# Paged attention taken two units at a time, with the rotary keys in a record of their own

## The chip, the cores and the metric

The kernel runs on one core of a Trainium2 chip. The metric is the time of one execution on the device in microseconds (us); three runs of the kernel before took 2031.20, 2032.12 and 2036.46 us, so its median is 2032.12 us. The engines named below are PE (the matrix engine, with PEld for its weight loads), DVE (vector), ACT (scalar), POOL (GpSimd) and SP, whose queue only issues transfers here.

## The reference

The reference is one inference step of a two-layer decoder: 1024 prompt tokens and 64 sample tokens (8 sequences of 8 tokens). The change lies in the attention of the sample tokens in layer 1. Each sequence has a past of 8192 keys, kept in 64 pages of 128 keys that a page table picks out of a pool of 640. A key has 256 latent features (`ckv`), 64 rotary features (`kpe`) and one factor for each of the 8 heads (`ks`):

```python
def mla_scores(q_abs, q_pe, ckv, kpe, ks):
    s = (jnp.einsum('bqhc,bkc->bhqk', q_abs, ckv) + jnp.einsum('bqhr,bkr->bhqk', q_pe, kpe))
    return s * (jnp.transpose(ks, (0, 2, 1))[:, :, None, :] * SM_SCALE)

def step(carry, pages):                       # over blocks of pages, for all sequences b
    m, l, acc = carry
    ck, kp, kk = cache_ckv[pages], cache_kpe[pages], cache_ks[pages]
    s = mla_scores(q_abs, q_pe, ck, kp, kk)
    m_new = jnp.maximum(m, jnp.max(s, axis=-1))
    alpha = jnp.exp(m - m_new)
    p = jnp.exp(s - m_new[..., None])
    l = l * alpha + jnp.sum(p, axis=-1)
    acc = acc * alpha[..., None] + jnp.einsum('bhqk,bkc->bhqc', p, ck)
    return m_new, l, acc
```

## The kernel before

Two streams of work are written by generators and merged by `interleave` (line 1780) into one fixed program order: after each step of the right stream (`fr`, line 1816), steps of the left stream (`fl`, line 1817) are emitted until their estimated costs, the numbers after `yield`, have caught up. Every engine and every queue then runs its own part of that order strictly from front to back. While the right stream does the paged attention (`samp_attn`, line 1051), the left one does the dense work of 768 prompt tokens: layer 0's projections, its output product, and layer 1's projections. It streams weight units (`Stream`, line 276): SP loads a unit two ahead (line 297), ACT and DVE or POOL split it in two parts one ahead (lines 183 and 179), PE uses it in products of 384 columns (lines 189 to 191).

The paged attention has 64 units of 8 pages (512 keys). For a unit `u`:

- `load_rec` (line 1060) has SP read the 8 page numbers from `PTi` into registers (line 1064) and then issue 8 transfers from the page pool (line 1067), one for a page. A page's record holds 128 rows of 384 numbers, 1536 bytes a row: 2 x 128 latent columns, 64 columns of rotary keys (64 features of keys 0 to 63 in the lower 64 rows, of keys 64 to 127 in the upper ones), and 64 columns of key factors. There are `RECB` = 2 buffers of 8 records, so the transfers of unit `u + 2` wait until unit `u` has been combined.
- `scores` (line 1080) makes three pairs of f32 products, each with 128 rows and 64 columns of the array and 512 columns streamed: two over the latent (line 1087), one over the rotary part (line 1089), whose query tile `QPE` has zeros in the 64 rows that don't belong. The two of a pair stand for keys 0 to 63 and 64 to 127 of each page and go to the lower and the upper 64 partitions of one bank.
- `combine` (line 1092, DVE) multiplies by the key factors and takes the running maximum; it is the last reader of the record. `soft` (line 1102, ACT) takes the exponentials once for two units (`CU` = 2).
- `tr` and `trev` (lines 1121 and 1128) transpose the weights on PE and copy them out on ACT; `pv` (line 1137) multiplies them with rows of the latent that POOL gathers by indirect transfers (`load_nat`, line 1069); `pvend` (line 1154) adds to the accumulator. A unit's `tr` and `pv` come two units after its scores.

The loop at line 1193 does, for each `u`: loads of `u + 2`, scores of `u`, a step of other work, `combine`, transposes of `u - 2`, a small step, `soft` for every second unit, `pv` of `u - 2`, a step of other work. Order on SP is thus page loads of one unit, then whatever loads and stores the left stream has emitted, then the page loads of the next unit.

## Time and profile before

| what | value |
|---|---|
| median of three runs | 2032.12 us (2031.20 to 2036.46) |
| the profiled execution: its span, from first to last instruction | 2030.3 us |
| PE busy over the span | 1934.9 us (95%) |
| DVE, ACT, POOL busy over the span | 979.2, 744.7, 669.5 us (48%, 37%, 33%) |
| DMA queue that SP feeds | 172178 packets, 298.75 MB, 44.7% of 16 engines |
| DMA queue that POOL feeds | 20528 packets, 67.26 MB, 10.2% of 16 engines |

The profile's page doesn't count the issuing of transfers as busy time of SP; SP is read from the rows of single lines and of the timeline. A line such as `L1067` is line 1067 of the kernel. In lines with instruction durations the three numbers are the least, the median and the greatest in ns.

### The profile page before, as it was taken

What the parts mean: (1) busy time and instruction counts of PE and PEld (TensorE: products, weight loads), DVE (VectorE), ACT (ScalarE), POOL (GpSimd) and SP (SyncE); (2) the same over time, 40 slices, a digit from 0 to 9 for tenths busy, and PEclk for the clock granted to TensorE, in tenths of its full rate; (3) what the DMA queues carried; (4) which work ended last, traced back from release to release, by engine and by line L of the source; (5) the groups of instructions that cost most, each with busy time, mean ns of one, the idle gap of its engine ahead of it and who ended that gap; (6) DMA issues with size and microseconds to landing.
All of it is one profiled execution on the core that took longest, in us unless ns stands there. A gap on an engine that the chain in (4) does not pass through costs nothing. (4 is left out here: it accounts for less than half of the span.)

```text
span 2030.3 us, 33997 instructions
## 1 busy us (share of the span) xinstructions
PE 1934.9 (95%) x11740; PEld 1619.7 (80%) x11740; DVE 979.2 (48%) x2450; ACT 744.7 (37%) x1499; POOL 669.5 (33%) x589
## 2 busy tenths in 40 slices
PE   6997999999999999999999999999998899999999
PEld 5987998998997867667777765777687687787999
DVE  7659444456644533444323443344456656657300
ACT  6434323333321223333222322333333666667300
POOL 4544433422220223233434324333333334433220
PEclk8999999999999999999999999999999999999999
DMA  6552535442535487687988878877852311114532
GB/s 222 168 198 94 179 117 197 145 143 88 176 131 194 136 266 247 226 303 242 339 298 273 278 259 271 264 254 235 270 178 70 93 57 58 59 46 129 179 96 73
DMA packets 192877, 368.17 MB, mean 181 GB/s; under 512 B 27809, under 2 KB 135585, under 8 KB 191426
## 3 DMA queue, kind: packets, MB, share of 16 engines
q1 hardware_dynamic: 172178, 298.75, 44.7%
q0 software_dynamic: 20528, 67.26, 10.2%
q8 instruction: 93, 1.52, 0.3%
q14 instruction: 78, 0.64, 0.1%
HBM read 331.22 MB, written 34.70 MB: 180 GB/s over the span
## 5 line engine op out<-in xcount | busy, mean ns | idle before, releaser
L1078 POOL DMA_INDIRECT nat<-nat,IX x256 | 274.2, 1071 | 490.4 <-PE pv L1152 422.0
L189 PE MATMUL mm<-xH,whi 128*128 128x384 f32 (+1 forms) x1112 | 372.4, 335 | 9.7 <-ACT whi L183 5.1
L191 PE MATMUL mm<-xH,wli 128*128 128x384 f32 (+1 forms) x1112 | 367.1, 330 | 6.1 <-POOL wli L179 4.2
L190 PE MATMUL mm<-xL,whi 128*128 128x384 f32 (+1 forms) x1112 | 366.9, 330 | 0.8 <-DVE xL L179 0.8
L189 PEld LDWEIGHTS mm<-xH,whi 128*128 128x128 f32 x1112 | 213.8, 192 | 32.2 <-issue 13.3
L183 ACT ACTIVATE whi<-wri 128x1024 fp32r<-128x1024 f32 (+1 forms) x130 | 126.1, 977 | 271.1 <-PE mm L190 202.6
L191 PEld LDWEIGHTS mm<-xH,wli 128*128 128x128 f32 x1112 | 213.6, 192 | 8.3 <-POOL wli L179 5.3
L190 PEld LDWEIGHTS mm<-xL,whi 128*128 128x128 f32 x1112 | 213.8, 192 | 4.1 <-issue 2.4
L179 POOL TENSOR_TENSOR wli<-wri,whi 128x1024 fp32r<-128x1024 f32 (+1 forms) x65 | 146.9, 2264 | 161.2 <-ACT whi L183 161.0
L1087 PE MATMUL sAB<-rec,qar 128*64 128x512 f32 x512 | 153.5, 602 | 0.4 <-DMA rec<-rec 0.2
L1152 PE MATMUL pv<-nat,PT 128*64 128x256 f32 x1024 | 140.9, 392 | 4.8 <-ACT PT L1132 4.0
L1152 PEld LDWEIGHTS pv<-nat,PT 128*64 128x64 f32 x1024 | 75.6, 138 | 55.4 <-issue 13.5
L179 DVE TENSOR_TENSOR wli<-wri,whi 128x1024 fp32r<-128x1024 f32 (+1 forms) x65 | 72.8, 1124 | 72.1 <-ACT whi L183 69.9
L189 PE MATMUL mm<-nH,whi 128*128 128x384 f32 x304 | 105.6, 347 | 0.5 <-issue 0.5
L190 PE MATMUL mm<-nL,whi 128*128 128x384 f32 x304 | 102.4, 338 | 0.0
L191 PE MATMUL mm<-nH,wli 128*128 128x384 f32 x304 | 102.3, 337 | 0.0
L179 POOL TENSOR_TENSOR wlo<-wro,who 128x768 fp32r<-128x768 f32 (+3 forms) x30 | 59.2, 1978 | 118.0 <-ACT who L183 117.9
L189 PE MATMUL mm<-yHo,who 128*128 128x384 f32 (+1 forms) x288 | 97.1, 337 | 0.9 <-ACT yHo L183 0.9
L183 ACT ACTIVATE who<-wro 128x768 fp32r<-128x768 f32 (+3 forms) x44 | 38.1, 873 | 155.9 <-PE mm L190 117.7
L191 PE MATMUL mm<-yHo,wlo 128*128 128x384 f32 (+1 forms) x288 | 94.3, 327 | 0.0
L190 PE MATMUL mm<-yLo,who 128*128 128x384 f32 (+1 forms) x288 | 93.9, 326 | 0.0
L1089 PE MATMUL sAB<-rec,QPE 128*64 128x512 f32 x256 | 91.2, 596 | 0.0
(595 smaller groups left out, 4336.9 us busy)
## 6 DMA issues: line engine op xcount, KB each, us to landing
rec<-rec SPq DMA_DIRECT2D x512, 192.0 KB
wri<-wi SPq DMA_DIRECT2D x114, 512.0 KB
wro<-wo SPq DMA_DIRECT2D x29, 384.0 KB
smkv<-ckm SPq DMA_DIRECT2D x16, 512.0 KB
smkv<-cvm SPq DMA_DIRECT2D x16, 512.0 KB
wrm<-memw SPq DMA_DIRECT2D x7, 1024.0 KB
wro<-wo SPq DMA_DIRECT2D x7, 768.0 KB
yld<-d_ys SPq DMA_DIRECT2D x8, 544.0 KB
```

What stands on the lines that cost most here:

```text
L179: eng.tensor_tensor(out=out, in0=a, in1=h.bitcast(F), op=ALU.subtract)
L183: A.activation(h, src, AF.Copy)
L189: T.matmul(out, wh, xh, start=first, stop=False)
L190: T.matmul(out, wh, xl, start=False, stop=False)
L191: T.matmul(out, wl, xh, start=False, stop=last)
L1078: G.indirect_dma_start(out=t[:, j % 2, :], out_offset=None, in_=I["nat"], in_offset=bass.IndirectOffsetOnAxis(ap=IX[:, q:q + 1], axis=0), ...
L1087: T.matmul(o, QA[:, cb, b, :], t[:, :, cb * 128 + ab * 64:cb * 128 + ab * 64 + 64], start=(cb == 0), stop=False)
L1089: T.matmul(o, QPE[:, b, ab, :], t[:, :, 256:320], start=False, stop=True)
L1152: T.matmul(d["v"][64 * ab:64 * ab + 64, 0:256], PT[:, j, ab, :], n[j][:, ab * 256:ab * 256 + 256], start=(i == 0 and j == 0), stop=(i == C ...
```

## The change

- The record of a page loses its rotary columns: 128 rows of 320 numbers (1280 bytes). The rotary keys become a tensor of their own, `kpr`, with 64 rows of 128 keys (512 bytes a row) for each page.
- `load_rec` issues two transfers for each page: 64 rows of `kpr` into the lower half (first unit of a pair) or the upper half (second unit) of a tile that both units of the pair share, and then the record. There are three buffers of records (`RECB` = 3) and two of the new tile. The load of unit `u + 3` is written behind `combine` of unit `u`.
- `scores` takes both units of a pair: the latent products of the first, those of the second (each as before), and then the four rotary products, each with 64 rows and 64 columns: rows 0 to 63 for the first unit, rows 64 to 127 for the second, two column halves each, into the two units' own banks. `QPE` holds the same queries in both halves, without zeros.
- The loop runs over 32 pairs: scores of both, other work, `combine` and next page load for both, `soft` (now always ahead of the transposes), a small step, transposes and copies of both units of the pair before, a small step, `pv` of both with the gathers that reuse their buffers, other work. The costs after `yield` are those of two units before (5.5 + 0.5 + 0.5 + 4.5 against twice 3.0 + 0.5 + 2.0).
- The second unit's transposes use a bank of the tag `s`; the page table is kept in the spare partition of the tile of own-key weights; the scratch that POOL's indirect transfers use is set to 2048 bytes a partition.
- The comments that the diff removes are left out here.

```diff
-RECB = 2
+RECB = 3
@@ samp_prep
-        QPE = pk.tile([128, DB, 2, 64], F, name="QPE")
-        G.memset(QPE, 0.0)
-        PsT = pk.tile([NS, DB, NS], F, name="PsT")
+        QPE = pk.tile([128, DB, 64], F, name="QPE")
+        PsP = pk.tile([128, DB * NS], F, name="PsP")
+        PsT = PsP[0:NS].rearrange("p (b k) -> p b k", b=DB)
...
-        PTi = pk.tile([1, DB * NPG], I32, name="PTi")
+        PTi = PsP[NS:NS + 1, :].bitcast(I32)
...
-        V.tensor_copy(QPE[0:64, :, 0, :], qpf)
-        A.activation(QPE[64:128, :, 1, :], qpf, AF.Copy)
+        V.tensor_copy(QPE[0:64], qpf)
+        A.activation(QPE[64:128], qpf, AF.Copy)
@@ samp_attn, load_rec
+            c, j = u // CU, u % CU
             with tc.issue_after(regs["last"]):
                 v = nc.values_load_multi_w_load_instructions(PTi[0:1, 8 * u:8 * u + 8], engines=[ET.SP], min_val=0, max_val=NPOOL - 1)[1]
-            t = raw[u] = prec.tile([128, 8, 384], F, name="rec", tag="rec", bufs=RECB)
+            if j == 0:
+                kpr[c] = prec.tile([128, 8, 128], F, name="kpr", tag="kpr", bufs=2)
+            t = raw[u] = prec.tile([128, 8, 320], F, name="rec", tag="rec", bufs=RECB)
             for i in range(8):
+                S.dma_start(out=kpr[c][64 * j:64 * j + 64, i, :], in_=I["kpr"][bass.ds(v[i], 1), :, :].rearrange("o p f -> (o p) f"))
                 regs["last"] = S.dma_start(out=t[:, i, :], in_=I["rec"][bass.ds(v[i], 1), :, :].rearrange("o p f -> (o p) f")).ins
@@ scores
-        def scores(u):
-            b = u // UB
-            s = pst("s", "sAB")
-            t = raw[u]
-            for cb, ab in ((cb, ab) for cb in range(3) for ab in range(2)):
-                o = s[64 * ab:64 * ab + 64, :]
-                if cb < 2:
-                    T.matmul(o, QA[:, cb, b, :], t[:, :, cb * 128 + ab * 64:cb * 128 + ab * 64 + 64], start=(cb == 0), stop=False)
-                else:
-                    T.matmul(o, QPE[:, b, ab, :], t[:, :, 256:320], start=False, stop=True)
-            return s
+        def scores(c, kp):
+            b = CU * c // UB
+            ss = [pst("s", "sAB") for _ in range(CU)]
+            for j, s in enumerate(ss):
+                t = raw[CU * c + j]
+                for cb in range(2):
+                    for ab in range(2):
+                        T.matmul(s[64 * ab:64 * ab + 64, :], QA[:, cb, b, :], t[:, :, cb * 128 + ab * 64:cb * 128 + ab * 64 + 64], start=(cb == 0), stop=False)
+            for j, s in enumerate(ss):
+                q = slice(64 * j, 64 * j + 64)
+                for ab in range(2):
+                    T.matmul(s[64 * ab:64 * ab + 64, :], QPE[q, b, :], kp[q, :, 64 * ab:64 * ab + 64], start=False, stop=True)
+            return ss
@@ tr
-            tp = pst("t", "ptp")
+            tp = pst("s" if i else "t", "ptp")
@@ the loop
-        load_rec(0)
-        load_rec(1)
-        load_nat(0)
+        for u in range(RECB):
+            load_rec(u)
+        for u in range(CU):
+            load_nat(u)
         yield
-        for u in range(NU + LAG):
-            pu = u - LAG
-            load_rec(u + 2)
-            if u < NU:
-                s = scores(u)
-                yield 3.0
-                combine(u, s)
-                if u == NU - 1:
-                    RP.close(1)
-                    yield "T"
-            if pu >= 0:
-                load_nat(pu + 1)
-                PT = trev(pu, tr(pu))
-            yield 0.5
-            if u % CU == CU - 1 and u < NU:
-                soft(u // CU)
-            if pu >= 0:
-                pv(pu, PT)
-                yield 2.0
-                pvend(pu)
+        NC = NU // CU
+        for c in range(NC + 1):
+            us = range(CU * c, CU * c + CU)
+            pus = range(CU * c - CU, CU * c)
+            if c < NC:
+                ss = scores(c, kpr.pop(c))
+                yield 5.5
+                for u, s in zip(us, ss):
+                    combine(u, s)
+                    load_rec(u + RECB)
+                if c == NC - 1:
+                    RP.close(1)
+                    yield "T"
+                soft(c)
+            yield 0.5
+            if c:
+                PT = [trev(u, tr(u)) for u in pus]
+                yield 0.5
+            if c:
+                for u, x in zip(pus, PT):
+                    pv(u, x)
+                    load_nat(u + CU)
+                yield 4.5
+                pvend(pus[-1])
@@ prepare and kernel
-    rec = np.empty((NPOOL, 128, 384), np.float32)
+    rec = np.empty((NPOOL, 128, 320), np.float32)
...
+    a["kpr"] = C(i["cache_kpe"].transpose(0, 2, 1))
...
-    nc = _bacc.Bacc("TRN2", target_bir_lowering=False, num_devices=1)
+    nc = _bacc.Bacc("TRN2", target_bir_lowering=False, num_devices=1, dynamic_dma_scratch_size=2048)
```

## Rows read from the trace of the kernel before

**Rows 1.** Windows: PE, PEld, DVE, ACT, POOL busy, clock, DMA share, GB/s.
```profile
700.00:1455.00 755.00, 743.67 (x4294) 530.18 (x4293) 301.79 (x856) 239.54 (x566) 257.65 (x254) 0.99 0.81 267
```
**Rows 2.** Line 1067, the page transfers on SP: durations in ns, first and last start.
```profile
L1067 SPq FUSED_REGOPS  x512: 2/37/701, 698.3 to 1454.6; - x171
L1067 SPq MOVE rec<-rec x512: 3/29/676, 698.4 to 1454.7; - x171
L1067 SPq DMA_DIRECT2D rec<-rec x512: 2/333/1260, 700.3 to 1454.8; - x171
```
**Rows 3.** Timeline of SP: start, us, operation; page transfers of one unit and of two.
```profile
1070.30 3.96 SPq L1067 DMA_DIRECT2D rec<-rec  x8
...
1148.95 11.53 SPq L1067 DMA_DIRECT2D rec<-rec  x16
```
**Rows 4.** Waits of SP's queue, 700 to 1456 us: total, times, longest.
```profile
SPq L1067 <- DVE mx L1097: 52.1, 20, 8.1
...
SPq L440 <- ACT mqH L183: 0.2, 1, 0.2
```
**Rows 5.** Issues of one transfer on SP: 64 rows, 128 rows, 8 rows.
```profile
L882 SPq DMA_DIRECT2D d_kp<-kpT x8: 485/569/1248, 444.9 to 1272.7; - x8
...
L1253 SPq DMA_DIRECT2D lraw<-d_ck x2: 327/378/430, 1481.5 to 1518.6; - x2
...
L1253 SPq DMA_DIRECT2D lraw<-d_kp x1: 494/494/494, 1526.1 to 1526.1; - x1
...
L1329 SPq DMA_DIRECT2D aqr<-d_qp x8: 450/453/487, 1580.0 to 1775.6; - x8
...
L1374 SPq DMA_DIRECT2D out_ksT<-akt x8: 303/303/343, 1589.8 to 1845.2; - x8
```
**Rows 6.** Transfers issued from 700 to 1456 us; SP's first and last rows.
```profile
rec<-rec SPq DMA_DIRECT2D x512, 192.0 KB
wri<-wi SPq DMA_DIRECT2D x22, 512.0 KB
...
out_newc<-newc SPq DMA_DIRECT2D x1, 72.0 KB
```
**Rows 7.** From the page: splitting a weight unit on ACT and DVE.
```profile
L183 ACT ACTIVATE whi<-wri 128x1024 fp32r<-128x1024 f32 (+1 forms) x130 | 126.1, 977 | 271.1 <-PE mm L190 202.6
...
L179 DVE TENSOR_TENSOR wli<-wri,whi 128x1024 fp32r<-128x1024 f32 (+1 forms) x65 | 72.8, 1124 | 72.1 <-ACT whi L183 69.9
```
**Rows 8.** Lines 1097 (combine) and 1114 (exponentials): durations in ns.
```profile
L1097 DVE CUSTOM_DVE_ANT_1 ss<-sAB,rec,mx x56: 734/751/753, 723.3 to 1478.3; 128x512 f32<-128x512 f32 x56
...
L1114 ACT ACTIVATE ss<-ss,nb x64: 705/709/732, 725.5 to 1480.2; 128x512 f32<-128x512 f32 x64
```
**Rows 9.** Windows: a wait of PE at 1251.65 us, then two more stretches.
```profile
1250.00:1254.80 4.80, 2.35 (x14) 1.05 (x11) 2.79 (x14) 0.89 (x5) 2.34 (x3) 1.00 1.05 379
1254.80:1258.20 3.40, 3.40 (x14) 1.72 (x14) 0.89 (x6) 2.42 (x7) 0.00 (x0) 0.50 0.61 198
```
**Rows 10.** Timeline of PE around one unit's scores.
```profile
1004.96 0.33 PE L190 MATMUL mm<-yLo,who 128*128 128x384 f32 x1
1005.14 0.34 PE L191 MATMUL mm<-yHo,wlo 128*128 128x384 f32 x1
1005.41 1.95 PE L1152 MATMUL pv<-nat,PT 128*64 128x256 f32 x16
1007.18 1.89 PE L1087 MATMUL sAB<-rec,qar 128*64 128x512 f32 x8
1008.90 1.03 PE L1089 MATMUL sAB<-rec,QPE 128*64 128x512 f32 x4
1009.86 0.44 PE L189 MATMUL mm<-yHo,who 128*128 128x384 f32 x1
1010.14 0.34 PE L190 MATMUL mm<-yLo,who 128*128 128x384 f32 x1
```
**Rows 11.** Timeline of PE: products with 32 columns, four places side by side.
```profile
305.01 1.92 PE L586 MATMUL smo<-smkv,smPT 128*32 128x512 f32 x16
```

## The prediction

> **What bounds the kernel now.** I read the windows first. From 700 to 1455 us, the stretch in which the pages are loaded [rows 2], PE is busy for 743.67 of 755.00 us at a granted clock of 0.99, the other compute engines for less than half of it, and the transfer engines for 0.81 [rows 1]. So PE sets the time of this stage, and a unit of 8 pages takes (1454.8 - 700.3) / 64 = 11.8 us, most of it the prompt's dense products in between. The next question is who comes second, since the change works on PE but also doubles the number of page transfers. The windows don't show SP; its timeline and its waits do. Eight page transfers are issued in 3.96 us, and two units, with the reading of one unit's page numbers between them, in 11.53 us [rows 3]. That leaves 11.53 - 2 x 3.96 = 3.6 us for the page numbers, so a unit costs SP 3.6 + 4.0 = 7.6 us of its 11.8. For 64 units that is 484 us. The left stream's transfers on SP are 128 in this window (20 rows from the weight units to `out_newc` [rows 6]); at 0.45 us each, between the 0.30 and 0.57 that an issue takes [rows 5], they add 58 us. SP thus works some 543 us and, by the list of its waits (36 rows from 52.1 down to 0.2 us, 186 us in sum [rows 4]), waits for 186, nearly all for buffers to come free. That accounts for 729 of 755 us. SP is 72% full in the stage: this is the resource that the change loads.

> **The change, part by part.**

> *Page transfers.* Each page now takes two transfers, so SP issues 512 more in the stage. A page issue is 0.52 us after the one before ((3.96 - 0.34) / 7 [rows 3]), of which the transfer instruction is 0.33 and the rest, 0.19, goes to a register operation, a move and the gaps; both of these stand in the trace once for each transfer (x512 [rows 2]), and since the new tensor has another page size, its address needs them once more. The instruction itself has no row of this shape. The nearest are transfers of 64 rows: 0.57 us median with 512 bytes a row, though a store; 0.45 for a load with longer rows; 0.49 for another, where the same line's loads of 128 rows take 0.33 to 0.43. So 64 rows cost more than 128, not less. The cheapest issue of a few rows is 0.30 [rows 5]. I take 0.51, between the two nearest: 0.19 + 0.51 = 0.70 us, 512 x 0.70 = 358 us. The ends are 0.49 us (251 us in all) and 0.76 us (389 us). It can't be below nothing, as nothing is taken from the issues that are there. With the 543 us, SP has 901 us of work (794 to 932) in a stage of 755. No cover hides it: the waits of 186 us are eaten first, and the stage then lasts as long as SP works, 146 us more (39 to 177).

> *What SP's bound adds.* Loads of a pair stand in a row, 2 x 13.2 = 26 us on SP, and the left stream's loads and stores queue behind them. A weight unit that is written behind such a block reaches SP only after it; its split on ACT and DVE (0.98 and 1.12 us [rows 7]) stands ahead of the next `combine` on DVE, and `combine` (0.75 us [rows 8]) is what frees the buffer that SP's next block waits for. In such a pair SP stands still for at least 0.98 + 1.12 + 0.75 = 2.9 us and the landing of the unit. The left stream gets 11.55 of its cost units for a pair and yields 7.7 for a weight unit, so about half of the pairs have a unit in that place. I take 1.5 us a pair, 48 us; the ends are 0 (the units fall elsewhere) and 5 us a pair, 160 us. [...]

> *Scores.* Starts of the products of one unit run from 1007.18 to 1009.86 us for 12 instructions, two side by side: six slots of 0.43 us, two of them rotary [rows 10]. For a pair that is four rotary slots; after, the eight rotary instructions use the four quarters of the array. If four run side by side, they need two slots, and 2 x 0.43 x 32 = 27 us of PE go away; if only two do, nothing. Four side by side are there with 32 columns: 16 instructions of 512 columns in 1.92 us, 4 slots [rows 11]; no row shows two row halves at work. I take 27.

> *Changes of shape on PE.* Into the products of 64 columns the start comes 0.27 us after the one before instead of 0.18; out of them it is 0.10 late, and the next product another 0.10 [rows 10]: 0.3 us a visit. Before there are 64 to 128 visits (where `pv` runs into the scores, as in these rows, two are one), after at most 64: 0 to 19 us saved, I take 10. [...]

> *Order on ACT.* `soft` of the pair now stands ahead of the copies that `pv` of the pair before needs. Two `combine` (1.5 us) and two exponentials (1.4 us [rows 8]) can come between the transposes and `pv`, where before the copy came first: 0 to 2 us a pair, I take 0.8, 25 us of PE. On its own PE thus gains 27 + 10 - 25 = 12 us (46 at best, and at worst it loses 64). All of it lies under SP's bound and doesn't count there.

> *Edits with one answer.* The bytes are the same (1280 + 256 against 1536 a row), the transfer engines have room at 0.81, a third buffer of records lets SP start earlier but adds no issue speed, the gathers on POOL are the same 256, and `QPE` and the page table are set up once.

> **The sum.** 2030.3 us (the profiled span) + 146 + 48 = 2224 us. The median of the runs is 1.8 us above that span, so 2226 us. [...]

> **The rivals.**

> *A. The issues hide, and PE decides (the other side).* SP absorbs the new transfers in its 186 us of waits. This needs 186 / 512 = 0.36 us for each, less than any issue in the rows with its register work (0.49). It holds if the addresses of both transfers are worked out in one go and the instruction for 64 short rows is as quick as that for 8: 0.30 + gaps of 0.05. Then the time is 2032 - 12 = 2020 us, 1986 at best. Chance 0.10. [...]

> *B. Issues hide nearly, and the new order on PE and ACT costs more than the scores save.* The rotary products run two by two (no 27 us), and `pv` waits 2 us a pair for `soft`: 64 - 10 = 54 us, 2086 us. For it speaks that `pv` and the copy are close neighbours now; against it that other work is written between them. Also here lies the SP bound at its cheap end (39 us, 2071). Chance 0.08.

> *C. The change doesn't do what it says*, the four rotary products running in pairs, is no case of its own: under SP's bound it changes nothing, and under A it gives 2047 us.

> **How the numbers follow.** The forecast, SP's queue sets the stage, has 0.82. Its own span is 2071 (cheap issues, no coupling) to 2326 (2032 + 177 + about 117 of the 160 us of coupling). The range for 8 in 10 is 2055 to 2330: it holds nine tenths of the forecast's chance and most of B. A measurement of this kernel can tell 0.3%, 6 us, from no change. Faster: A without its poorer part, 0.07. Same: the rest of A and a little of B, 0.04. Slower: the forecast and B, 0.89.

> **What would show it.** In the profile after, 512 transfers of the new tensor on SP at 0.45 to 0.57 us each; SP's waits for buffers down from 186 to well under 100 us although the stage is longer; PE waiting at the first scores of a pair for a page transfer, some 150 to 250 us in sum, with PE's busy share of the stage near 0.8 and stretches at half clock; the stage at some 950 us instead of 755, and the DMA share down to about 0.65. Four rotary starts within a slot would show the scores right. Wrong would be a new issue that takes under 0.36 us, register work and all, or SP waits that stay at 186 us.

## The result, and the profile after

The changed kernel takes 2287.55 us (median; 2284.24 to 2292.81) against 2031.66 us for the kernel before: 1.1275 times as long, 95% interval 1.1249 to 1.1301, which is 256 us more. The forecast was 2226 us with a range of 2055 to 2330, so the sign and the mechanism held and the size fell short by 61 us.

The windows show where the time is. The stretch in which pages are loaded (columns as in [rows 1]):

```profile
703.00:1714.00 1011.00, 832.09 (x4319) 542.17 (x4319) 302.26 (x855) 241.20 (x564) 252.26 (x257) 0.91 0.65 200
```

The stage now lasts from 704 to 1714 us, 1010 instead of 755 us, and that is the whole difference. PE does the same work (4319 instructions for 4294), but its share falls to 0.82, its granted clock from 0.99 to 0.91 and the share of the transfer engines from 0.81 to 0.65 [rows 1]. No engine of the windows is fuller than before, so the cause is one that they don't show. SP's lines (least, median and greatest ns; first and last start), to be read beside [rows 2]:

```profile
L1072 SPq DMA_DIRECT2D kpr<-kpr x512: 2/475/1643, 703.3 to 1713.2; - x171
L1073 SPq DMA_DIRECT2D rec<-rec x512: 3/446/1791, 704.1 to 1713.9; - x171
```

The 512 new transfers take 0.475 us each in the median. The old ones have become dearer too: 0.446 us, where they took 0.333. SP's timeline has the rhythm, one page every 1.29 us where it was 0.52 [rows 3]:

```profile
1068.88 0.48 SPq L1072 DMA_DIRECT2D kpr<-kpr  x1
1069.55 0.43 SPq L1073 DMA_DIRECT2D rec<-rec  x1
1070.17 0.48 SPq L1072 DMA_DIRECT2D kpr<-kpr  x1
```

SP's list of waits has shrunk from 36 rows with 186 us [rows 4] to 22 with 25 us, of which this is the first. Below it the first rows of PE's list (total us, times, longest), of 33 with 178 us, where PE had waited for 11 us in the whole stage before:

```profile
SPq L297 <- DMA wri<-wi: 3.6, 1, 3.6
```

```profile
PE sAB L1093 <- DMA rec<-rec: 67.0, 17, 7.1
PE sAB L1093 <- issue: 36.3, 13, 6.2
PE pv L1160 <- ACT PT L1140: 26.1, 25, 4.9
```

The waiting has moved from SP to PE, and the largest row of it ends with the landing of pages; "issue" marks waits whose end the trace ties to nothing. A wait before the scores has a second price, seen in the windows around one of them (one that the trace ties to nothing) and, below, in PE's timeline:

```profile
1080.00:1083.50 3.50, 0.00 (x0) 0.00 (x0) 0.00 (x0) 0.00 (x0) 2.26 (x3) 0.93 0.87 263
1083.50:1087.00 3.50, 3.42 (x9) 1.03 (x10) 0.96 (x1) 0.84 (x1) 2.06 (x2) 0.59 1.04 419
```

```profile
1083.58 3.32 PE L1093 MATMUL sAB<-rec,qar 128*64 128x512 f32 x8 [4.45 <-issue]
```

PE idles for 4.45 us, comes back at half clock (0.50 from 1083.50 to 1086.00 us, as after the wait in [rows 9]), and its first eight instructions take 3.32 us instead of 1.89 [rows 10].

One thing is not in the program text: the compiled order of each engine's instructions isn't the order in which the program emits them, so the order told above for the loop holds for the program alone. In the changed kernel the pair's products are taken apart again, and no four of the 128 rotary products stand together (54 groups of two, 20 single ones; a product of f32 is two instructions, as the x8 below for a unit's four latent products shows). In the trace a unit's rotary products stand alone:

```profile
1101.76 1.94 PE L1093 MATMUL sAB<-rec,qar 128*64 128x512 f32 x8
1103.62 1.08 PE L1097 MATMUL sAB<-kpr,QPE 64*64 64x512 f32 x4
1104.63 0.66 PE L1133 MATMUL ptp<-ident,ss 128*128 128x128 f32 x4
```

### The profile page after: what moved, and what is told of

Its sections match the earlier page's. It is cut to its first block, busy times and chain, and to the rows that moved or that the text cites. A ratio compares the mean times of both kernels' runs of the same rounds, so it can differ in the third digit from the quotient of the medians.

```text
span 2291.0 us, 35434 instructions
## 1 busy us (share of the span) xinstructions
PE 2018.1 (88%) x11740; PEld 1627.7 (71%) x11740; DVE 982.8 (43%) x2450; ACT 746.6 (33%) x1499; POOL 660.0 (29%) x588
## 5 line engine op out<-in xcount | busy, mean ns | idle before, releaser
L1084 POOL DMA_INDIRECT nat<-nat,IX x256 | 266.3, 1040 | 741.3 <-PE pv L1160 665.5
L1093 PE MATMUL sAB<-rec,qar 128*64 128x512 f32 x512 | 166.0, 749 | 111.2 <-DMA rec<-rec 67.0
L189 PEld LDWEIGHTS mm<-xH,whi 128*128 128x128 f32 x1112 | 214.0, 192 | 31.6 <-issue 11.8
L1160 PE MATMUL pv<-nat,PT 128*64 128x256 f32 x1024 | 141.1, 403 | 41.6 <-ACT PT L1140 26.1
L1093 PEld LDWEIGHTS sAB<-rec,qar 128*64 128x64 f32 x512 | 41.1, 161 | 178.9 <-issue 166.9
L1105 DVE CUSTOM_DVE_ANT_1 ss<-sAB,rec,mx 128x512 f32<-128x512 f32 x56 | 42.0, 750 | 205.9 <-PE sAB L1097 184.6
L1140 ACT ACTIVATE PT<-ptp 128x512 f32<-128x512 f32 x64 | 37.8, 595 | 212.3 <-PE ptp L1133 197.1
```

The lines of the kernel that those rows point to most:

```text
L189: T.matmul(out, wh, xh, start=first, stop=False)
L1084: G.indirect_dma_start(out=t[:, j % 2, :], out_offset=None, in_=I["nat"], in_offset=bass.IndirectOffsetOnAxis(ap=IX[:, q:q + 1], axis=0), ...
L1093: T.matmul(s[64 * ab:64 * ab + 64, :], QA[:, cb, b, :], t[:, :, cb * 128 + ab * 64:cb * 128 + ab * 64 + 64], start=(cb == 0), stop=False)
L1105: V.tensor_tensor_reduce(out=ss.rearrange("p (g k) -> p g k", g=8), in0=s.rearrange("p (g k) -> p g k", g=8), in1=raw.pop(u)[:, :, 256:320 ...
L1140: A.activation(PT, src, AF.Copy)
L1160: T.matmul(d["v"][64 * ab:64 * ab + 64, 0:256], PT[:, j, ab, :], n[j][:, ab * 256:ab * 256 + 256], start=(i == 0 and j == 0), stop=(i == C ...
```

## The experiments

All ratios are to the kernel before, run on the same chip (there it took 2029.7, 2022.0, 2023.2 and 2024.3 us). Where SP's work is given, it is counted from all of its instructions between the first and the last page transfer: their durations and the gaps to the next up to 0.12 us; what is left is its idle time. By this count SP works 531 us and idles 223 us before, and works 930 and idles 80 us after. It takes every instruction of the trace, so no single line of a view shows it.

The runs stand on four chips. The first four (issues alone, another queue, one transfer a page twice) ran on one chip, the other eight on three more. The traces of these two groups differ, which matters further down.

**Issues alone.** The kernel before, its loop untouched, with an extra transfer for each page that nobody reads:

```diff
+            if j == 0:
+                kpr[c] = prec.tile([128, 8, 128], F, name="kpr", tag="kpr", bufs=2)
...
             for i in range(8):
+                S.dma_start(out=kpr[c][64 * j:64 * j + 64, i, :], in_=I["kpr"][bass.ds(v[i], 1), :, :]...)
                 regs["last"] = S.dma_start(out=t[:, i, :], in_=I["rec"][bass.ds(v[i], 1), :, :]...)
```

> The kernel before with nothing changed but SP's work: each page also gets the 64-row transfer of the new tensor, into a tile that no instruction reads; scores, record and loop are as before. Theory (SP's queue sets the stage): SP has 543 us of work before; 512 more issues at the 0.45 to 0.70 us that the profile after shows (0.475 median for the instruction, 0.13 to 0.19 around it) make 850 to 900 us in a stage of 755, so 2130 to 2200 us, and up to 2290 if buffers wait as they do in the changed kernel. Rival (the pair order on PE, ACT and the s banks costs the time, and the issues hide in SP's 186 us of waits): 2025 to 2045 us.

2256.6 us, ratio 1.111 (1.106 to 1.116). The transfers alone cost 0.111 x 2031.7 = 226 of the 256 us. SP works 929 and idles 62 us, PE has the picture of the changed kernel, and the record's issue is as dear as there. Its window of the stage, and SP's two lines:

```profile
707.00:1699.00 992.00, 813.71 (x4400) 559.04 (x4398) 304.18 (x861) 242.01 (x566) 263.89 (x263) 0.92 0.71 221
```

```profile
L1071 SPq DMA_DIRECT2D kpr<-kpr x512: 2/475/1986, 706.8 to 1697.9; - x171
...
L1072 SPq DMA_DIRECT2D rec<-rec x512: 3/446/1787, 707.6 to 1698.5; - x171
```

**The rotary keys by another queue.** The changed kernel, its rotary keys fetched by 8 of POOL's indirect transfers a pair, so that SP issues records alone:

```diff
-                S.dma_start(out=kpr[c][64 * j:64 * j + 64, i, :], in_=I["kpr"][...])
...
+        def load_kpr(c):
...
+            for i in range(8):
+                G.indirect_dma_start(out=t[:, i, :], out_offset=None, in_=I["kpr"], in_offset=bass.IndirectOffsetOnAxis(ap=IXK[:, 8 * c + i:8 * c + i + 1], axis=0), ...)
```

> The changed kernel, but the rotary keys of a pair come by eight indirect transfers on POOL (128 rows, one page of each unit), not by sixteen on SP; everything else is the changed kernel's. Theory: SP is back at some 540 us, PE decides again: 1985 to 2040 us. Rival (the pair order costs the time): 2200 us or more. A second rival (the gathers queue on POOL behind those that wait for the products with the weights): some 2050 to 2150 us, with PE waiting for the new tile.

2219.5 us, ratio 1.0967 (1.0914 to 1.1019): above what either the theory or the second rival allowed, and by its number in the range of the first rival, the pair order. SP has room again (work 564, idle 334 us), but the time is not back: another queue has taken its place. POOL, busy for 258 us in this stage before [rows 1], now is for 501. The window of the stage:

```profile
714.00:1613.00 899.00, 766.19 (x4199) 531.73 (x4197) 291.63 (x829) 230.97 (x546) 501.04 (x489) 0.92 0.71 221
```

And the first rows of the waits of POOL (total us, times, longest):

```profile
POOL kpr L1081 <- PE sAB L1105: 123.0, 26, 18.5
POOL nat L1092 <- PE pv L1168: 117.1, 32, 12.8
```

In its gathers POOL waits 240 us for PE to release their buffers (the two rows above), which with the 501 us makes 741 of the stage's 899. So this run decides neither for SP nor for the pair order: it moves work to another queue, which then fills. The next two runs decide. It shows one other thing, four rotary products abreast: a pair's eight instructions start within two slots, as many as the changed kernel's trace needs for the four of one unit:

```profile
1008.89 3.65 PE L1101 MATMUL sAB<-rec,qar 128*64 128x512 f32 x16
1012.48 1.09 PE L1105 MATMUL sAB<-kpr,QPE 64*64 64x512 f32 x8
```

**One transfer a page, twice.** First the record widened to 448 columns with the rotary keys in both halves, so that the pair loop and the quarter products stay but a page is one transfer again; then, in the same pair loop, the record of the kernel before (384 columns) with its rotary products. The edit of the first:

```diff
-t = raw[u] = prec.tile([128, 8, 320], F, name="rec", tag="rec", bufs=RECB)
+t = raw[u] = prec.tile([128, 8, 448], F, name="rec", tag="rec", bufs=RECB)
-S.dma_start(out=kpr[c][64 * j:64 * j + 64, i, :], ...)
...
-T.matmul(s[64 * ab:64 * ab + 64, :], QPE[q, b, :], kp[q, :, 64 * ab:64 * ab + 64], start=False, stop=True)
+T.matmul(s[64 * ab:64 * ab + 64, :], QPE[q, b, :], raw[CU * c + j][q, :, 320 + 64 * ab:384 + 64 * ab], start=False, stop=True)
```

> The changed kernel with one transfer a page: the record holds the 64 rows of rotary keys twice, in the lower and the upper half (448 numbers a row), and the rotary products read it there. SP's issues are those of the kernel before, the bytes a page grow by 17%. Theory: 1985 to 2040 us. Rival (the pair order costs the time): 2200 us or more. Rival (bytes): the transfer engines, at 0.81 before, get 50 us more work, and the time is above 2050 us.

> The changed kernel's loop and buffers with the record, the zero-padded queries and the rotary products of the kernel before: only the order of the work and the third buffer differ from before. Theory: no new issues, so near 2032 us: 2010 to 2060 us (10 us saved by fewer changes of shape, up to 60 us lost where the copy waits for the exponentials). Rival (the pair order costs the time): 2200 us or more. Against e3 it gives the worth of rotary products in quarters of the array: 27 us if four run side by side, none if two do.

2081.1 us, ratio 1.0271 (1.0227 to 1.0316), and 2098.8 us, ratio 1.0342 (1.0297 to 1.0388). With SP out of the way (539 and 549 us of work in 780 and 805) most of the loss is gone, which agrees with the first experiment and rules out the rival of 2200 us. The bytes of the wide record aren't what keeps its time above 2050 us, since the run without them is no faster. But both times lie above what was expected: in these runs the pair loop isn't the small gain that the prediction made of it, alone it costs 69 us. The quarter products give 0.0071 of that back, 14 us with an uncertainty as large. PE's waits in the stage are 54 us in sum over 20 rows, none above 7.1, and the clock is 0.96 where it was 0.99 [rows 1]. The wide record's window, and its three largest waits of PE:

```profile
703.00:1484.00 781.00, 725.74 (x4199) 512.67 (x4196) 291.79 (x830) 228.45 (x546) 245.46 (x249) 0.96 0.82 276
```

```profile
PE pv L1157 <- ACT PT L1137: 7.1, 3, 4.2
PE ckt L874 <- DVE kr L796: 6.5, 3, 5.1
PE ckt L873 <- DVE ckn L859: 6.1, 2, 4.4
```

**Why the record's issue became dearer.** The changed kernel, with the eight rotary transfers of a unit first and then its eight records:

```diff
             for i in range(8):
                 S.dma_start(out=kpr[c][64 * j:64 * j + 64, i, :], ...)
+            for i in range(8):
                 regs["last"] = S.dma_start(out=t[:, i, :], ...)
```

> The changed kernel with the two kinds of page transfer no longer alternating on SP: the 8 of the rotary keys of a unit first, then the 8 of its records. Same transfers, same loop. In the changed kernel the issue of a record takes 0.446 us in the median, before 0.333, and the two together take 1.29 us with their register work. Theory (alternating shapes make the record's issue dearer): it falls back to about 0.33, SP loses 512 x 0.11 = 58 us of work, and since SP sets the stage the time falls from 2288 to about 2230 us. Rival 1 (the issue is dearer because the record's row is now 1280 bytes, or because more transfers are under way): it stays at 0.44 and the time at about 2288 us. Rival 2 (the first record waits behind eight rotary transfers, or the other way round, so pages come together later): 2288 to 2310 us.

2213.4 us, ratio 1.0957 (1.0922 to 1.0992): 0.0318 or 65 us (56 to 74) less than the changed kernel, for the same transfers. The record is back at 0.333 us, as SP's lines show:

```profile
L1072 SPq DMA_DIRECT2D kpr<-kpr x512: 468/469/1475, 702.1 to 1625.6; - x171
...
L1074 SPq DMA_DIRECT2D rec<-rec x512: 332/333/1709, 708.5 to 1630.4; - x171
```

So the dearer issue comes from the alternation of the two kinds of transfer, not from the record's shorter rows. The time that comes back, 65 us, is about the 58 us expected, but not all of it is the issues': of SP's stage, 46 us go from its work (930 to 884), of which the records' issues are 37 in sum (223 to 186), and 36 from its idle time (80 to 44). The idle time is dealt with under the exponentials.

**Half of the new transfers, and the place of the exponentials.** Four kernels belong together. One brings rotary keys with 256 transfers of 128 rows instead of 512 of 64 (the second unit of a pair gets the keys of the wrong page):

```diff
+                if j == 0:
-                S.dma_start(out=kpr[c][64 * j:64 * j + 64, i, :], in_=I["kpr"][bass.ds(v[i], 1), :, :]...)
+                    S.dma_start(out=kpr[c][:, i, :], in_=I["kpr"][bass.ds(v[i], 2), :, :]...)
```

> The changed kernel with half of its additional transfers: one of 128 rows for each page of a pair's first unit, which brings rotary keys for both halves of the tile, 256 instead of 512. Left out: the second unit's rotary keys are those of the neighbouring page in the pool, not its own. Theory (a threshold: SP costs time only where its work exceeds the stage): SP's work is about 543 + 256 x 0.55 = 684 us, under the 755 of the stage, so PE sets it again, and what is left is the loss of the pair order with one transfer a page (2081 with four rotary products abreast, 2099 with them in pairs): 2080 to 2120 us. Rival (every issue costs, as the pages' lateness grows with SP's load): half of 256 us on top of 2032, 2160 us or more.

Three have the exponentials where they stood before the change, behind the transposes and copies: the wide record, the changed kernel, and the one with half of the transfers.

```diff
-                soft(c)
             yield 0.5
             if c:
                 PT = [trev(u, tr(u)) for u in pus]
+            if c < NC:
+                soft(c)
+            if c:
                 yield 0.5
```

> The wide record with one transfer a page and the pair order (2081 us), with the exponentials of a pair written behind the transposes and copies of the pair before, as before the change, instead of ahead of them. Theory (the pair order loses because the second products wait on ACT for copies behind the exponentials, 25 us in the prediction): 2050 to 2062 us, and PE's waits for copies of the transposed weights nearly gone. Rival (the loss is that both units' work on DVE and ACT comes in one block, so the left stream's splits wait): 2075 to 2090 us, with PE's waits spread as they were.

> The changed kernel with only the exponentials of a pair moved behind the transposes and copies of the pair before. With one wide transfer a page this move took the ratio to the kernel before from 1.027 to 0.996. Theory (SP's queue sets the stage of the changed kernel, so what PE and ACT lose or gain lies under it): ratio 1.115 to 1.130, against 1.1275 of the changed kernel. Rival (the order on ACT costs beside SP's queue, and the two add): 1.09 to 1.10.

> The changed kernel with half of its additional transfers (256 of 128 rows instead of 512 of 64 rows) and with the exponentials written behind the transposes and copies of the pair before. Left out as in the other kernel with half of them: the second unit's rotary keys are those of the neighbouring page in the pool. Theory (an issue costs time only from the point at which SP's work fills the stage; SP's work was 671 us with half of the issues): what the move of the exponentials gives with one transfer a page is given here too, ratio 0.988 to 1.002. Rival (issues cost from the first one on, as pages come later): 1.010 to 1.030, that is, no better than the 1.013 with the exponentials ahead.

| new transfers on SP | exponentials ahead | exponentials behind | SP's work, idle (behind) |
|---|---|---|---|
| none (wide record) | 1.0271 | 0.9956 (0.994 to 0.9971) | 534, 188 us |
| 256 of 128 rows | 1.0133 (1.0105 to 1.0161) | 1.0093 (1.0061 to 1.0125) | 667, 84 us |
| 512 of 64 rows | 1.1275 | 1.1115 (1.1079 to 1.1152) | 929, 41 us |

Down the column with the exponentials behind (the first row's kernel also moves 17% more bytes), 256 transfers cost 0.0137 (28 us) and 512 cost 0.1159 (235 us). That is far from proportional, as a queue that fills up gives it, but it isn't the sharp threshold expected either: with SP working 667 of 752 us something is already lost, PE waits for 31 us in sum, and the ratio of 1.0093 is out of the theory's range and next to the rival's. In the new transfers of 128 rows the issue takes 0.333 us for both kinds, though they alternate as well:

```profile
L1073 SPq DMA_DIRECT2D kpr<-kpr x256: 332/333/1215, 701.8 to 1444.0; - x128
...
L1074 SPq DMA_DIRECT2D rec<-rec x512: 332/333/1654, 702.5 to 1457.4; - x171
```

Across the rows, the kernels with the exponentials behind are faster by 0.0315 (64 us, 54 to 74) with one transfer a page, by 0.0160 (32 us) under SP's bound, and by 0.0040 with 256 transfers, with an uncertainty as large. Whether the place of the exponentials does this isn't shown, because in no row are the two kernels known to have run on one chip, and their traces differ in more than the edit. An instruction of SP that has nothing to wait for, the range check of a page number, shows it (least, median and greatest ns); the changed kernel first, then the same with the exponentials behind:

```profile
L1067 SPq SEQ_ASSERT  x512: 1/18/710, 588.7 to 1703.2; - x171
```

```profile
L1067 SPq SEQ_ASSERT  x512: 18/18/28, 587.3 to 1661.9; - x171
```

The traces of the kernel before, of the changed kernel and of the four runs on the first chip all look like the first line, those of the eight runs on other chips all like the second. The six also have idle time on DVE and ACT that ends with a release from outside the core's own records ("remote"): 19 us in the stage of the kernel before, 202 us with the wide record. The eight have none. The six traces are called disturbed from here on. The largest such row of the wide record:

```profile
DVE xr L765 <- remote: 46.6, 8, 8.3
```

The first and the third row of the table thus compare a disturbed trace with an undisturbed one; only the second, with its 0.0040, compares two undisturbed ones. So there is a rival that no run tests: a good part of the 0.0315 and of the 0.0160 goes with the chip and not with the edit. It would also explain why 256 more transfers seem to make the kernel faster in the column with the exponentials ahead, and why two of the four runs, 2013.0 us for the wide record with the exponentials behind and 2048.9 for 256 transfers with them ahead, came out below their expected ranges (2050 to 2062 and 2080 to 2120), which were worked out from times of the first chip. Under SP's bound the idle time of SP falls from 80 to 41 us with its work unchanged, but not because SP waits less for others: its list of waits rises from 25 to 47 us. Idle time between two register instructions, where nothing is waited for, falls from 33 to 4 us, as it does with the grouped issues.

With one transfer a page and the exponentials behind, PE's waits fall from 54 to 26 us in sum and the clock rises to 0.99. The wide record's window again, now with the exponentials behind, and the first row of PE's waits:

```profile
703.00:1426.00 723.00, 696.14 (x4209) 499.58 (x4209) 294.16 (x829) 228.66 (x548) 249.08 (x249) 0.99 0.87 299
```

```profile
PE pv L1157 <- ACT PT L1137: 7.8, 5, 4.1
```

But the wait that the theory named, that of `pv` for the copies, is as long as it was (7.8 us against 7.1), and under SP's bound it is longer with the exponentials behind (36.8 us against 26.1). So the named mechanism is not what the traces show, and where the 64 us come from stays open.

**Scores in pairs, all else by units.** The loop of the kernel before, with three buffers of records and scores of two units in a row: with the wide record and quarter products, and with the record and the rotary products of the kernel before. And the kernel before with the third buffer alone.

```diff
-            load_rec(u + 2)
...
+                if u % CU == 0:
+                    ss = scores(u // CU)
-                s = scores(u)
                 yield 3.0
-                combine(u, s)
+                combine(u, ss[u % CU])
+                load_rec(u + RECB)
```

> The wide record with one transfer a page, the scores of two units in a row with their four rotary products abreast, but everything else by single units in the loop and with the steps of the kernel before (combine, transposes, exponentials, second products, 3.0 + 0.5 + 2.0). Theory (the loss of the pair order lies in the blocks of two units behind the scores, not in the scores themselves): PE gains the 18 us of the rotary products, 2010 to 2025 us, which would beat the kernel before. Rival (scores in pairs are the harm: pages of two units must be there at once, and the second unit's bank is held for half a pair longer): 2050 to 2090 us. If neither the loop nor the scores harm and the wide record does (bytes 17% up, transfers at 0.8 and more): about 2060 us with PE waiting for pages.

> The kernel with scores in pairs and the rest by units, but with the record of the kernel before (384 numbers a row) and its rotary products: 128 rows with zeros, two side by side, eight slots of 0.43 us where the four abreast take two of 0.48 in place of four of 0.43 a pair. Theory (the scores in pairs cost nothing by themselves, and the quarter products are worth 0.76 us a pair, 24 us of PE): ratio 1.000 to 1.005, some 0.010 above the 0.991 of the version with quarters. Rival (the gain is that of the scores in a row, with fewer changes of shape on PE): 0.990 to 0.994.

> The kernel before with three buffers of records instead of two, the load of unit u + 3 behind the combine of unit u, and the smaller scratch of the indirect transfers that makes room for it; nothing else. The kernel with scores in pairs has these as well and runs at 0.991 of before. Theory (its gain comes from four rotary products abreast): 0.997 to 1.003, SP's waits for the combine of a unit shorter, PE at 0.98 of the stage as before. Rival (the gain is the third buffer's, which hides late pages): 0.988 to 0.994.

Ratios 0.9909 (0.9876 to 0.9941), 0.9968 (0.9948 to 0.9988) and 1.0004 (0.9987 to 1.0021). The third buffer shows no effect by itself. Scores in a row with it give 0.0032, 6.5 us, where none was expected. The quarter products add 0.0059 (12 us, 4 to 20) where 0.010 was expected: 28 of the 32 pairs have them four abreast in the compiled order. The first of these three takes 2002.26 us against 2022.01 for the kernel before on the same chip, a small gain but outside the uncertainty. The window of its stage, and one pair's scores in PE's timeline:

```profile
703.00:1416.00 713.00, 700.47 (x4237) 510.69 (x4238) 296.88 (x840) 234.03 (x552) 253.63 (x249) 1.00 0.88 304
```

```profile
1105.18 2.79 PE L1090 MATMUL sAB<-rec,qar 128*64 128x512 f32 x10
1107.90 1.09 PE L1094 MATMUL sAB<-rec,QPE 64*64 64x512 f32 x8
```

The clock is at 1.00, and the transfer engines at 0.88: the bytes of the twice stored rotary keys are hidden here, where the issues of the changed kernel are not.

## Why the prediction was right, and where its sizes were off

*SP's queue sets the stage: right, and shown.* The signs asked for are all there: new transfers at 0.45 to 0.57 us (0.475), SP's waits well under 100 us (25), PE waiting for 150 to 250 us in sum (178), PE's share near 0.8 (0.82), stretches at half clock (0.50 from 1083.50 to 1086.00 us), transfer share 0.65. What carries the verdict is the first experiment, 226 of 256 us from the issues alone, and the wide record, which takes the transfers away and four fifths of the loss with them (0.1275 to 0.0271). It holds without the disturbance as well: with the exponentials behind, in an undisturbed trace, SP works 929 and idles 41 us of the stage, and the ratio is 1.1115.

*SP's work, forecast 901 us, counted 930.* The new transfers were put at 0.70 us each with their register work, 358 us. Their issues take 0.475 us in the median and 244 us in sum, and register work with its gaps rose by 116 us: 360 us, so this term was right. The failed term is the one that wasn't there: the old transfers' own issue rose by 0.113 us in the median, 46 us in sum (177 to 223). That "nothing is taken from the issues that are there" was said of a gain; that something could be added to them was left out. The work before was 531 and not 543 us, and the other transfers took 7 us less: 901 + 2 + 46 - 12 - 7 = 930.

*What SP's bound adds, forecast 48 us (0 to 160).* SP still idles for 80 us of the changed stage, and that is the remainder: 930 + 80 = 1010. The term was 32 us too small, and its mechanism, SP kept waiting for buffers through the splits of weight units, is shown for a part at most: 25 us stand in the list of waits. 33 us are idle time between two register instructions of SP, which the prediction didn't have and which are 4 us in the undisturbed traces; the remaining 20 us or so have no releaser, and stay open. That the number came within its bounds is thus partly luck. The two errors, 29 and 32 us, are the 61 us by which the stage is longer than the 949 us that the sum made of it.

*The scores, forecast 27 us less on PE.* In the changed kernel they don't run four abreast at all, as the compiled order separates the units. Where they do, they are worth 12 us (4 to 20). The forecast had no row for the step from 128 x 64 to 64 x 64 and put nothing for it. The rows of the result have it: the four latent slots before the rotary ones last from 1101.76 to 1103.62, 1.86 us, where they lasted 1.72 [rows 10]. Of the 0.14 us more, 0.05 is the first slot behind another change of shape, which these rows of before don't have, and the rest, 0.10, is the step itself; the first rotary slot behind it is 0.05 us longer as well. The step thus costs some 0.15 us a pair, 5 of the 27 us; for 28 of 32 pairs 19 us are left, which the measurement allows. That four quarters work side by side is shown by the eight instructions in 1.09 us.

*Order on ACT, 25 us (0 to 64), and PE's gain of 12 us on its own.* This step isn't borne out in its mechanism: `pv` waits for the copies no longer with the exponentials ahead than behind (7.1 against 7.8 us with one transfer a page, 26.1 against 36.8 us in the changed kernel). What it is worth in time lies between 0.0040, with an uncertainty as large, and 0.0315 (8 and 64 us), and in no row is the chip known to be the same. With the exponentials behind the pair loop does gain: 0.9956, 9 us, near the 12 forecast (27 + 10 - 25) but made of other numbers, so that is luck. Whether all of it lies under SP's bound, as the prediction has it, is open: 32 us of difference come through there, and 29 of the 39 us that SP idles less lie between its register instructions.

*The rivals.* A, the issues hide, fell with the first experiment: an issue costs 0.475 + 0.19 us where 0.36 were to be had. B, issues nearly hidden and an order that costs, isn't what happened; the pair loop with one transfer a page comes to its 2086 us within 13 us (2081 and 2099), but without the wait of `pv` that B made it from. C was the case and, as said, no case of its own. The price of the issues, with the exponentials behind: 256 transfers of 128 rows at 0.333 us cost 28 us, 512 of 64 rows at 0.475 cost 235. In the changed kernel, where a page is issued every 1.29 us, what costs is SP's queue, while the transfer engines are at a share of 0.65.

## What to carry to other kernels

Before splitting a transfer in two, count what its queue already does in the stage that it runs in: the windows didn't show SP, and it was 70% full. If the data can be stored so that one transfer brings both, even with bytes twice, do that, as long as the transfer engines have room (here 1.0271 instead of 1.1275, at a transfer share of 0.82). Where a compiler or planner orders the engines, look up the compiled order before crediting a loop with an order of products. And when two kernels differ by a few per cent, run both on one chip and compare in their traces an instruction that has nothing to wait for, before the edit gets the credit: the 3% of the exponentials here can't be told from the change of chip.

- An issue of 128 rows takes 0.333 us in a row of its own kind and 0.446 us when it alternates with issues of 64 rows; alternating with another kind of 128 rows it stays at 0.333. The issue of 64 rows takes 0.475 alternating and 0.469 in a row of eight. An issue of 64 rows is thus dearer here than one of 128, and makes its neighbour dearer; it isn't a rule of fewer rows, as one of 8 rows took 0.303 [rows 5].
- Four quarters of 64 x 64 do run side by side. The first slot of 512 columns behind a change of shape takes 0.48 us, with 128 x 64 and with 64 x 64; later ones of 128 x 64 take 0.43, and the step from 128 x 64 to 64 x 64 adds 0.10 (medians of some 50 places each in the changed kernel's trace).
- Waits of PE come with a lower clock and longer work: from 26 to 54 us of waits in the stage (the wide record, exponentials behind and ahead) the clock goes from 0.99 to 0.96 and PE's busy time from 696 to 726 us; with 178 us of waits the clock is 0.91.
- One and the same register instruction of SP (the range check) lasts 18 to 28 ns in eight traces, and from 1 or 2 to over 700 ns in six. No run shows whether the chip does this, and whether it is in the engine or only in its record.
